# Layer 0 of a two-layer hybrid kernel: one double of seven products fewer, two value blocks beside the attention, deeper mLSTM rings, output weights in the projections' slabs

## The chip, the cores and the metric

The kernel runs on one core of a Trainium2 chip. The metric is the device time of one execution in microseconds (us), as the median of several executions. A profile of one execution has the order and the duration of every instruction on that core.

## What is computed

A backbone of two layers over 1024 latent tokens and 256 context tokens (1280 rows in all, width 1024), in float32. Layer 0 projects the modulated input h by one weight matrix `w_in_ab`, and runs two branches beside each other: 16 heads of neighbourhood attention, and 4 heads of a bidirectional mLSTM. Both are gated, joined and projected out.

```python
def _ab_mixer(h_lat, h_ctx, w_in, ...):
    qa, ka, va, za, qb, kb, vb, ob, zb, g = split(h @ w_in)
    oa_l = _neighbourhood_attention(qa_l, ka_l, va_l, ka_c, va_c, rpb)
    hb_l, hb_c = _mlstm_bidir(mb_l, mb_c, need_ctx)
    ...
    ya = oa * silu(za)
    yb = rms(hb * sigmoid(ob)) * silu(zb)
    return concatenate([ya, yb], -1) @ w_out
```

Layer 1 is a bidirectional gated recurrence (HGRN2) with its own projections. The change is in layer 0 alone; layer 1 takes the profiled execution from about 1900 us on.

## The kernel before, in words

**Precision.** Every float32 operand of a projection is split into a high and a low part (`split`, L72 to L75: ScalarE casts the high part, VectorE subtracts for the low part), and each product is three matmuls (L127 to L129 in `dense`, L743 to L745 in the output projection).

**Blocks.** A projection makes 256 columns at a time. `proj_out` (L269) makes a plain block: 10 token tiles by 8 slices of the depth by 3 matmuls of 128x256, so 240 matmuls; it is called for values (`na_values`), and by `ml_ahead` for the mLSTM's v, o and z. Its output goes through a tile `ev` and a DMA on POOL's queue to DRAM (`vd`, `md`). `q_seven` makes two blocks (a "double") from seven products of half-sized quarters, in Strassen's manner: 7 x 5 x 4 x 3 = 420 matmuls in place of 480, for more work on VectorE.

**Stages of layer 0, in order.** Modulation and h (`hh`, `hl`, kept on chip); gates and a few plain blocks; `a_ahead` with five doubles, the first for the values of attention heads 8 to 15 (the name "n"), the others for q and k of the mLSTM; the attention, in eight passes `p2` of two heads each; the mLSTM (`ml_all`, `ml_rec`), 25 steps g in which head h does its chunk g - 5h, so that one or two heads run at a time; the first half of the output projection's depth (`out_some`), beside the mLSTM; the rest of the output projection with layer 1's norm.

**Fillers.** PE's instructions are issued in program order, and that order is fixed when the program is built: a list scheduler places each instruction by its priority and by a simulated timeline. The plain blocks that nobody needs yet are given beside the attention and the mLSTM, where they stand between the small matmuls of these. Beside the attention this is the table `ahead` (which block after which pass), beside the mLSTM the constants `ML_AHEAD` (block z of head 3 from step 0) and `ML_OUT` (first tile of column half 1 at step 10, of half 0 at step 19, two tiles a step). The context manager `filler` gives them the lowest priority; `tc.issue_after` keeps them behind a certain instruction.

**Memory.** Weight slabs (`w`) and raw loads (`wraw`, 3 buffers) are in the pool `wa` on the right side, behind h. For the output projection `right.close()` at step 9 gives up h and slabs together, and the pool `oy` (weights `wo` in 8 buffers, raws `woraw` in 4, y tiles, accumulators) takes their place. All loads of weights and y tiles go through SP's queue, in order. The ring sizes of `ml_rec` (last argument of `self.t`) set how far a step's work may run ahead.

Of the kernel before, what the change touches and what calls it, by code (L numbers as in the profile page):

```python
# [9 lines left out]
F32 = mybir.dt.float32  # L10
# [8 lines left out]
P = 128  # L19
D = 1024  # L20
# [8 lines left out]
ML_AHEAD = {0: ("z", 3)}  # L29
ML_ORDER = [8, 9, 4, 5, 6, 7, 0, 1, 2, 3]  # L30
ML_OUT = (10, 19)
# [15 lines left out]
class Prog:  # L47
# [400 lines left out]
    def ml_rec(self, h, i, seqs, st, pool):  # L448
        nc = self.nc
        C, hs = st["C"], st["hs"]  # L450
        for d in range(2):
# [11 lines left out]
            if i > 0 or i < NT - 1:  # L463
                cw = self.t(pool, [P, P], F32, "mcw", 2)
                nc.scalar.activation(cw, Gb, AF.Exp, scale=-1.0, bias=self.mpb[:, d, h, i : i + 1])
            if i > 0:
                qc = self.t(pool, [P, 2, P], F32, "mqc", 2)
                nc.vector.tensor_tensor(
                    out=qc, in0=st["q"][c], in1=cw.unsqueeze(1).to_broadcast([P, 2, P]), op=ALU.mult
                )  # L470
                for j in range(2):
                    nc.tensor.matmul(num, lhsT=qc[:, j, :], rhs=C[d][:, j, :], start=False, stop=(j == 1))
            if i < NT - 1:
                vw = self.t(pool, [P, 258], F32, "mvw", 2)
                nc.scalar.activation(vw, st["v"][c], AF.Copy, scale=Dm[:, lastc : lastc + 1])
                us = []
                for j in range(2):
                    u = self.ps("s", [P, 258])
                    nc.tensor.matmul(u, lhsT=st["k"][c][:, j * P : (j + 1) * P], rhs=vw, start=True, stop=True)
                    us.append(u)  # L480
                if i == 0:
                    C[d] = self.t(pool, [P, 2, 258], F32, "mC", 4)
                    for j in range(2):
                        nc.vector.tensor_copy(C[d][:, j, :], us[j])
                else:
                    for j in range(2):
                        nc.vector.scalar_tensor_tensor(
                            out=C[d][:, j, :], in0=C[d][:, j, :], scalar=cw[:, lastc : lastc + 1], in1=us[j],
                            op0=ALU.mult, op1=ALU.add,
                        )  # L490
# [488 lines left out]
    def na_sink(self, b):  # L979
        return lambda c, t, m, o: self.q_store(self.vd[:, (b + c) * 256 : (b + c + 1) * 256], t, m, o)  # L980

# [25 lines left out]
    def a_ahead(self, pool):  # L1007
# [8 lines left out]
        S = {}  # L1016
# [5 lines left out]
        todo = [("n", 2)] + [(p, h) for h in (0, 2) for p in "qk"]  # L1022
        cols = [[2 * D + h * 256 + c * 256 if p == "n" else (4 + "qkvoz".index(p)) * D + (h + c) * 256 for c in range(2)] for p, h in todo]
        sinks = [self.na_sink(h) if p == "n" else self.ml_sink(p, h, pool) for p, h in todo]
        us = [self.q_two(self.q_raw(pool, cols[i], ("11", "21")), S, sinks[i], pool) for i in range(2)] + [None] * 9
# [195 lines left out]
    def build(self):  # L1221
# [3 lines left out]
        with ExitStack() as es:  # L1225
# [92 lines left out]
            wx = right.enter_context(tc.tile_pool(name="wx", bufs=2, side="right"))  # L1318
            self.six = [(self.wp, "w", 4)] * 4 + [(wx, "w", 2)] * 2
            with tc.tile_pool(name="na", bufs=2) as pool, self.pp.phase(tq=1, s=2, acc=1):  # L1320
# [3 lines left out]
                ahead = {2: ["o1"], 3: ["z1"], 4: ["v2"], 5: ["o2"], 6: ["z2"], 7: ["v3", "o3"]}  # L1324
                for p2 in range(8):
# [3 lines left out]
                    for i, x in enumerate(ahead.get(p2, [])):  # L1329
                        with tc.issue_after(self.at[(3, 7)[i]]) if p2 == 7 else nullcontext():  # L1330
                            self.ml_ahead(x[0], int(x[1]))
                    if p2 < 7:
                        z = self.na_z(p2 + 1, pool)
            with tc.tile_pool(name="ml", bufs=2) as pool, self.pp.phase(s=2, acc=2):
                wq = {}
                self.mask = self.t(pool, [P, 2, P], F32, "mmask", 1)
                dma(out=self.mask, in_=a["mmask"])
                wo = lambda q, b, ring, *later: self.wblock(
                    None, "wo", [a["woab"][q * D : (q + 1) * D, b * 512 : b * 512 + 512]], 8, 512, raws, *later, ring=ring
                )  # L1340

                def part(b, tt):
                    self.out_some(wq[b], 0, [tt], self.yd, yp, acc if b else None)

                for g, at in self.ml_all(pool):
                    with self.filler(), tc.issue_after(at.ins):
                        if g in ML_AHEAD:
                            self.ml_ahead(*ML_AHEAD[g])
                        if g == 9:
                            right.close()  # L1350
                            self.six = None
# [3 lines left out]
                            raws = [yp, 4, "woraw"]  # L1355
                        for b, g0 in ((1, ML_OUT[0]), (0, ML_OUT[1])):
                            if g == g0:
                                wq[b] = wo(0, b, [(yp, "wo", 8)] * 8)
                            for tt in ML_ORDER[max(0, 2 * (g - g0)) : max(0, 2 * (g - g0) + 2)]:
                                part(b, tt)  # L1360
                w2 = wo(1, 1, [(yp, "wo", 8)] * 8)
# [8 lines left out]
            with tc.tile_pool(name="op0", bufs=2) as op, ExitStack() as wl:  # L1370
# [13 lines left out]
                wr.close()  # L1384
                right = es.enter_context(ExitStack())
# [213 lines left out]
```

## Time and profile before

| | us |
|---|---|
| median of 3 runs | 3556.39 (3549.15 to 3556.89) |
| the profiled execution | 3552.23 |
| its span, first to last instruction | 3550.4 |
| mean granted TensorE clock | 0.991 |
| 24,318 matmul passes in the span, PE busy | 3466.5 |

The doubles take about 260 to 545 us of the span, the attention about 530 to 1372, the mLSTM 1394 to 1775, the output projection with layer 1's norm runs on to 1904. A matmul of two float32 operands appears in the trace as two passes. PE's busy time counts a pass from its start to its modelled end (0.28 us for 128x256), and passes overlap; what a pass takes of PE is seen from the distance of starts.

### The profile page before, as it was taken

The numbers are of one execution on the slowest core, as the hardware profiler recorded it, in microseconds if no ns is written. First come the engines' busy times: TensorE is split into PE (matmuls) and PEld (weight loads), VectorE is DVE, ScalarE is ACT, GpSimd is POOL, SyncE is SP. The second block draws the span as 40 slices with busy tenths as digits, with TensorE's granted clock in tenths as the row PEclk, the third lists the DMA queues.
The fourth block names the chain that finished last, engine by engine and source line by source line (L and its number), as shares of the span: only waits on it lengthen the run. The fifth ranks groups of instructions, "written<-read, shape, count | busy, mean of one in ns | idle before, by whom it ended". The sixth has DMA issues, their size and how long they took to land.

```text
span 3550.4 us, 64785 instructions
## 1 busy us (share of the span) xinstructions
PE 3466.5 (98%) x24318; PEld 3140.5 (88%) x24318; DVE 2406.6 (68%) x6079; ACT 1596.0 (45%) x3690; POOL 529.2 (15%) x840
## 2 busy tenths in 40 slices
PE   8999999999999999899999999999999999999989
PEld 5899999989999989777878999989999999999877
DVE  4568875776666654667567766577777777767853
ACT  5532224555555543656437333344444444444431
POOL 3211121222222211211211111001000100000010
PEclk9999999999999999999999999999999999999999
DMA  7543342222322224544374222212111211211354
GB/s 236 169 161 98 95 125 61 70 69 69 91 83 77 79 84 142 164 132 144 122 253 150 101 102 102 83 34 60 60 48 51 63 48 48 60 60 48 108 173 126
DMA packets 372681, 359.71 MB, mean 101 GB/s; under 512 B 30104, under 2 KB 322904, under 8 KB 372240
## 3 DMA queue, kind: packets, MB, share of 16 engines
q1 hardware_dynamic: 328944, 248.25, 23.9%
q0 software_dynamic: 43424, 107.32, 8.8%
q8 instruction: 192, 3.15, 0.4%
q14 instruction: 121, 0.99, 0.1%
HBM read 274.00 MB, written 81.32 MB: 100 GB/s over the span
## 4 chain that ended last, share of the span: by engine, by line
PE 84%; issue 5%; DMA 4%; DVE 3%; ACT 2%; POOL 1%; SPq 0%; POOLq 0%; ACTq 0%; DVEq 0%
PE mm L129 14%; PE mm L128 14%; PE mm L127 14%; PE s L1129 6%; PE sa L128 3%; PE sa L127 3%; PE sa L129 3%; PE acc L689 2%; PE mm L743 2%; PE mm L745 2%; PE mm L744 2%; PE tr L669 2%; PE s L1174 1%; PE tr L129 1%; PE tr L128 1%
## 5 line engine op out<-in xcount | busy, mean ns | idle before, releaser
L127 PE MATMUL mm<-wh,hh 128*128 128x256 f32 x1980 | 567.0, 287 | 1.2 <-ACT wh L74 1.1
L128 PE MATMUL mm<-wl,hh 128*128 128x256 f32 x1980 | 567.7, 287 | 0.3 <-DVE wl L75 0.2
L129 PE MATMUL mm<-wh,hl 128*128 128x256 f32 x1980 | 565.6, 286 | 0.0
L129 PE MATMUL mm<-hh,wl 128*128 128x512 f32 (+1 forms) x1344 | 491.0, 365 | 0.0
L127 PE MATMUL mm<-hh,wh 128*128 128x512 f32 (+1 forms) x1344 | 485.2, 361 | 0.0
L128 PE MATMUL mm<-hl,wh 128*128 128x512 f32 (+1 forms) x1344 | 483.9, 360 | 0.0
L127 PEld LDWEIGHTS mm<-wh,hh 128*128 128x128 f32 x1980 | 378.2, 191 | 8.3 <-issue 4.0
L128 PEld LDWEIGHTS mm<-wl,hh 128*128 128x128 f32 x1980 | 378.8, 191 | 4.2 <-DVE wl L75 0.7
L129 PEld LDWEIGHTS mm<-wh,hl 128*128 128x128 f32 x1980 | 378.3, 191 | 3.6 <-issue 1.2
L74 ACT CAST wh<-wraw 128x512 fp32r<-128x512 f32 x272 | 167.3, 620 | 279.3 <-PE mm L128 121.7
L128 PEld LDWEIGHTS mm<-hl,wh 128*128 128x128 f32 x1344 | 254.0, 189 | 32.1 <-issue 0.2
L129 PEld LDWEIGHTS mm<-hh,wl 128*128 128x128 f32 x1344 | 253.9, 189 | 30.2
L127 PEld LDWEIGHTS mm<-hh,wh 128*128 128x128 f32 x1344 | 254.3, 189 | 29.4
L1120 ACT COPY gksel<-gK 128x512 f32<-128x512 f32 x224 | 147.0, 663 | 214.2 <-PE s L1129 205.0
L743 PE MATMUL mm<-woh,yh 128*128 128x512 f32 x544 | 223.0, 410 | 8.3 <-ACT woh L74 4.4
L745 PE MATMUL mm<-woh,yl 128*128 128x512 f32 x544 | 220.0, 405 | 0.2 <-DVE yl L75 0.2
L744 PE MATMUL mm<-wol,yh 128*128 128x512 f32 x544 | 220.2, 405 | 0.0
L75 DVE TENSOR_TENSOR wl<-wraw,wh 128x512 fp32r<-128x512 f32 x272 | 184.4, 687 | 43.7 <-ACT wh L74 38.1
L1129 PE MATMUL s<-gQ,gksel 128*128 128x128 f32 x1536 | 199.8, 276 | 0.0
L1129 PEld LDWEIGHTS s<-gQ,gksel 128*128 128x128 f32 x1536 | 192.4, 191 | 7.0
L74 ACT CAST wh<-b 128x512 fp32r<-128x512 f32 x136 | 84.5, 622 | 209.2 <-PE sa L129 96.2
L1150 DVE TENSOR_TENSOR gQ<-gQ,gT 128x256 f32<-128x256 f32 x384 | 143.7, 416 | 28.0 <-PE s L1129 28.0
(458 smaller groups left out, 8738.0 us busy)
## 6 DMA issues: line engine op xcount, KB each, us to landing
wraw<-yd SPq DMA_DIRECT2D x144, 256.0 KB
wraw<-in_wc_dram SPq DMA_DIRECT2D x128, 256.0 KB
md<-ev POOLq DMA_DIRECT2D x92, 256.0 KB, 2.8
wraw<-in_wab_dram SPq DMA_DIRECT2D x86, 256.0 KB
adar<-in_wada_dram POOLq DMA_DIRECT2D x32, 512.0 KB, 4.8
b<-in_wc_dram SPq DMA_DIRECT2D x64, 256.0 KB
vzd<-qo POOLq DMA_DIRECT2D x56, 256.0 KB, 2.5
b<-in_wab_dram SPq DMA_DIRECT2D x34, 256.0 KB
```

What stands on the lines that cost most here:

```text
L74: nc.scalar.copy(hi, x)
L75: nc.vector.tensor_tensor(out=lo, in0=x, in1=hi.bitcast(F32), op=ALU.subtract)
L127: mm(ps, lhsT=lh(k), rhs=rh(k), start=(first and k == 0), stop=False)
L128: mm(ps, lhsT=lh(k), rhs=rl(k), start=False, stop=False)
L129: mm(ps, lhsT=ll(k), rhs=rh(k), start=False, stop=(last and k == nk - 1))
L669: nc.tensor.transpose(pt[:nk, i, :], pr[:, o : o + nk], self.ident)
L743: mm(ps, lhsT=yh[:, k, :], rhs=w.h(kk), start=(kk == 0), stop=False)
L744: mm(ps, lhsT=yh[:, k, :], rhs=w.l(kk), start=False, stop=False)
L745: mm(ps, lhsT=yl[:, k, :], rhs=w.h(kk), start=False, stop=(kk == 8 * len(qs) - 1))
L1120: nc.scalar.copy(ksel.rearrange("p (b s i) -> p b s i", s=2, i=h), pick(K))
L1129: nc.tensor.matmul(pa[:, c, :].rearrange("p (b s i) -> p b s i", s=2, i=h), lhsT=ksel[:, c * P : (c + 1) * P], rhs=qp[:, c * nbc : (c + 1) ...
L1150: nc.vector.tensor_tensor(out=t[:, i, :, s, :], in0=t[:, i, :, s, :], in1=bc(tot), op=ALU.mult)
```

## The change

Six things change, all in layer 0.

1. `a_ahead` makes four doubles in place of five: the double of values ("n", 2) goes.
2. The values of blocks 2 and 3 (heads 8 to 15) are made as plain blocks, after passes 1 and 2 of the attention. The other fillers move back by one or two passes; o of head 3 moves from pass 7 into the mLSTM.
3. `ML_AHEAD`: o3 from step -1, z3 from step 2 (before: z3 from step 0). `ML_OUT` becomes a list of steps for every tile: half 1 from step 8 to 12, half 0 from step 13 to 24.
4. Rings of `ml_rec`: E 2 to 3, Dm 3 to 5, SD, cw, qc and vw 2 to 4.
5. The pool `wa` is opened below h, so that h is given up alone (`rh.close()`, at step 7 in place of 9). The slabs live on to the end of the output projection, and output weights go into a ring of 11 places: 4 slabs `w` and 7 `wo`; their raws into `wraw` (3 buffers).
6. The extra slabs `wx` stand on the left side beside the attention's pool.

```diff
-ML_AHEAD = {0: ("z", 3)}
+ML_AHEAD = {-1: ("o", 3), 2: ("z", 3)}
-ML_OUT = (10, 19)
+ML_OUT = {1: (8, 8, 9, 9, 10, 10, 11, 11, 12, 12), 0: (13, 14, 14, 15, 16, 17, 18, 20, 22, 24)}
...
-            E = self.t(pool, [P, P], F32, "mE", 2)
+            E = self.t(pool, [P, P], F32, "mE", 3)
-            Dm = self.t(pool, [P, P], F32, "mD", 3)
+            Dm = self.t(pool, [P, P], F32, "mD", 5)
-            SD = self.t(pool, [P, P], F32, "mSD", 2)
+            SD = self.t(pool, [P, P], F32, "mSD", 4)
...
-        todo = [("n", 2)] + [(p, h) for h in (0, 2) for p in "qk"]
+        todo = [(p, h) for h in (0, 2) for p in "qk"]
...
-            self.open_h(right)
             self.wp = right.enter_context(tc.tile_pool(name="wa", bufs=2, side="right"))
+            rh = right.enter_context(ExitStack())
+            self.open_h(rh)
...
-                ahead = {2: ["o1"], 3: ["z1"], 4: ["v2"], 5: ["o2"], 6: ["z2"], 7: ["v3", "o3"]}
+                ahead = {1: ["n2"], 2: ["n3"], 3: ["o1"], 4: ["z1"], 5: ["v2"], 6: ["o2"], 7: ["z2", "v3"]}
...
-                        with tc.issue_after(self.at[(3, 7)[i]]) if p2 == 7 else nullcontext():
-                            self.ml_ahead(x[0], int(x[1]))
+                        with tc.issue_after(self.at[(3, 6)[i]]) if p2 == 7 else nullcontext():
+                            self.na_values(int(x[1])) if x[0] == "n" else self.ml_ahead(x[0], int(x[1]))
...
-                wq = {}
+                wq, self.six = {}, [(self.wp, "w", 4)] * 4
+                with self.filler(), tc.issue_after(self.at[8]):
+                    self.ml_ahead(*ML_AHEAD[-1])
...
+                def wo(q, b, ring=None):
+                    if not ring:
+                        ring, self.six = self.six[:8], self.six[8:] + self.six[:8]
+                    src = a["woab"][q * D : (q + 1) * D, b * 512 : b * 512 + 512]
+                    return self.wblock(None, "wo", [src], 8, 512, ring=ring)
...
-                        if g == 9:
-                            right.close()
-                            self.six = None
+                        if g == 7:
+                            rh.close()
...
+                            self.six = self.six + [(yp, "wo", 7)] * 7
...
-                w2 = wo(1, 1, [(yp, "wo", 8)] * 8)
+                w2 = wo(1, 1)
...
                 wr.close()
+                right.close()
+                self.six = None
```

What it moves is seen in the order of instructions. On PE, at the end of the second attention pass (p2 = 1), these rows stood in a row before; `s` are scores, `tr` and `tq` transposes, `acc` the attention's sums, and a projection would be `mm`:

```order
L619 MATMUL s_9112<-akh_8602,aqs_8600 128x256
L620 MATMUL s_9112<-akl_8604,aqs_8600 128x256
L669 MATMUL tr_9100<-ident_73,aP_9082 96x128 x2
L669 MATMUL tr_9100<-ident_73,aP_9082 72x128
L557 MATMUL tq_9922<-ident_73,aqn_9915 128x128 x4
L669 MATMUL tr_9106<-ident_73,aP_9082 128x128 x2
L632 MATMUL s_9117<-akh_8602,aqs_8600 128x264
L633 MATMUL s_9117<-akl_8604,aqs_8600 128x264
L619 MATMUL s_9157<-akh_8601,aqs_8599 128x256
L620 MATMUL s_9157<-akl_8603,aqs_8599 128x256
```

In the changed program the end of the same pass reads so on PE (`mm_9648` is the q and k projection of a later pass, which now has its turn here since the block n2 was done earlier in the pass):

```order
L669 MATMUL tr_7892<-ident_73,aP_7870 96x128 x3
L128 MATMUL mm_9648<-wl_9464,hh_126 128x256
L669 MATMUL tr_7897<-ident_73,aP_7870 128x128 x2
L619 MATMUL s_7931<-akh_6843,aqs_6841 128x256
L620 MATMUL s_7931<-akl_6845,aqs_6841 128x256
L129 MATMUL mm_9648<-wh_9465,hl_127 128x256
L127 MATMUL mm_9648<-wh_9472,hh_126 128x256
L128 MATMUL mm_9648<-wl_9471,hh_126 128x256
L662 MATMUL acc_7889<-ident_73,arb_7887 128x128
```

The stretch without a projection, 67 rows long before (rows 5544 to 5611 of PE), is gone there. At the start of the last pass such a stretch stays, and goes from 89 rows (9080 to 9169) to 66 (8920 to 8986).

On PE, in the mLSTM, these rows are out of a stretch of 126 (10129 to 10255) that held no filler before; `num` is `acc`, `s` is a score or an update of the state, `tr` a transpose:

```order
L479 MATMUL s_19156<-mvw_19154,mkn_3104_18221 128x258
L479 MATMUL s_19158<-mvw_19154,mkn_3104_18221 128x258
L526 MATMUL tr_19178<-ident_73,mhs_3164_18374 128x128
L472 MATMUL acc_19227<-mC_18640,mqc_19231 128x258 x2
L394 MATMUL tr_19191<-ident_73,mqn_19189 128x128 x2
L479 MATMUL s_19237<-mvw_19235,mkn_3403_19004 128x258
L479 MATMUL s_19239<-mvw_19235,mkn_3403_19004 128x258
L400 MATMUL tr_19198<-ident_73,mkn_3475_19196 128x128 x2
```

In the changed program the same update of the state (its `mkn` has the number 18998 here) stands between matmuls of a tile of the output projection (`mm_19334`):

```order
L744 MATMUL mm_19334<-wol_19328,yh_19335 128x512
L462 MATMUL acc_19412<-mv_3004_17797,mSD_19410 128x258
L472 MATMUL acc_19412<-mC_17742,mqc_19416 128x258
L526 MATMUL tr_19177<-ident_73,mhs_3133_18368 128x128
L472 MATMUL acc_19412<-mC_17742,mqc_19416 128x258
L462 MATMUL acc_19449<-mv_2997_17779,mSD_19447 128x258
L526 MATMUL tr_19132<-ident_73,mhs_3144_18396 128x128
L472 MATMUL acc_19449<-mC_17767,mqc_19453 128x258
L479 MATMUL s_19238<-mvw_19234,mkn_3372_18998 128x258
L472 MATMUL acc_19449<-mC_17767,mqc_19453 128x258
L479 MATMUL s_19264<-mvw_19262,mkn_3379_19016 128x258
L745 MATMUL mm_19334<-woh_19329,yl_19336 128x512
```

Before, two long stretches of the mLSTM stood without a filler (126 and 118 rows, the second 10600 to 10718). In the changed program the longest is 37 rows (10229 to 10266), and fourteen shorter ones of 10 to 30 rows lie between there and the end of the mLSTM.

On SP's queue, where the output projection starts, this stood before; `gbc` is a row of gates that goes into the pool `oy`, and so waits until h is given up:

```order
L428 DMA mGb_3316_18764<-Gd_67 128x512 x2
L790 DMA gbc_22651<-gated_63 128x512 x2
L389 DMA mv_3399_18993<-md_72 128x256
L103 DMA woraw_19630<-in_woab_dram 128x512
L103 DMA woraw_19636<-in_woab_dram 128x512
L103 DMA woraw_19642<-in_woab_dram 128x512
L103 DMA woraw_19648<-in_woab_dram 128x512
L730 DMA wraw_19679<-yd_65 128x4x128
L730 DMA wraw_19683<-yd_65 128x4x128
```

In the changed program three of the weight loads stand some 30 rows ahead of it, and the rest about it:

```order
L103 DMA wraw_19306<-in_woab_dram 128x512
L790 DMA gbc_22643<-gated_63 128x512
L515 DMA mlz_19168<-md_72 128x256
L790 DMA gbc_22643<-gated_63 128x512
L103 DMA wraw_19312<-in_woab_dram 128x512
L103 DMA wraw_19318<-in_woab_dram 128x512
L415 DMA mkn_3445_19195<-md_72 128x256
L730 DMA wraw_19337<-yd_65 128x4x128
L730 DMA wraw_19341<-yd_65 128x4x128
```

More of the change, by code (lines that the diff above doesn't have):

```diff
@@ L1317, in build @@
                 self.a_ahead(pool)
-            wx = right.enter_context(tc.tile_pool(name="wx", bufs=2, side="right"))
-            self.six = [(self.wp, "w", 4)] * 4 + [(wx, "w", 2)] * 2
-            with tc.tile_pool(name="na", bufs=2) as pool, self.pp.phase(tq=1, s=2, acc=1):
+            with tc.tile_pool(name="na", bufs=2) as pool, tc.tile_pool(name="wx", bufs=2) as wx, self.pp.phase(tq=1, s=2, acc=1):
+                self.six = [(self.wp, "w", 4)] * 4 + [(wx, "w", 2)] * 2
                 qk = self.na_qk(0, pool)
```

30 lines of the change are left out of this document (11 added, 19 removed).

## The prediction

> **What bounds the kernel now.** I read the page's table of engines first, then the busy time by stretch, then the groups of PE and the order of time in the stretches that stand out.
>
> ```profile
> PE 3466.5 (98%) x24318; PEld 3140.5 (88%) x24318; DVE 2406.6 (68%) x6079; ACT 1596.0 (45%) x3690; POOL 529.2 (15%) x840
> ```
>
> PE bounds the kernel; VectorE (DVE) and ScalarE (ACT) have room on the mean. But 98% is no measure of what is left, since passes overlap. So I count passes by stretch. The columns are the stretch in us, its length, busy us and count for PE, PEld, DVE, ACT and POOL, then the granted clock and DMA.
>
> ```profile
> 350.00:400.00 50.00, 50.00 (x424) 50.00 (x422) 41.38 (x84) 10.14 (x17) 8.03 (x12) 1.00 0.31 96
> 740.00:780.00 40.00, 40.00 (x368) 38.66 (x366) 25.19 (x84) 18.52 (x52) 9.04 (x12) 1.00 0.25 66
> 780.00:812.00 32.00, 26.55 (x200) 22.56 (x201) 24.97 (x88) 19.54 (x59) 8.52 (x11) 0.84 0.26 79
> 812.00:850.00 38.00, 38.00 (x305) 34.68 (x300) 25.68 (x80) 21.06 (x55) 7.70 (x11) 1.00 0.36 99
> 1240.00:1288.00 48.00, 48.00 (x401) 44.18 (x399) 30.26 (x97) 23.33 (x64) 8.29 (x12) 1.00 0.28 81
> 1288.00:1313.00 25.00, 18.00 (x130) 13.41 (x127) 16.13 (x70) 9.06 (x33) 5.51 (x9) 0.86 0.34 97
> 1395.00:1460.00 65.00, 63.03 (x444) 59.08 (x445) 31.87 (x105) 30.98 (x89) 6.91 (x15) 1.00 0.44 140
> 1460.00:1533.00 73.00, 60.28 (x289) 46.51 (x288) 57.91 (x201) 50.27 (x151) 19.60 (x51) 0.95 0.66 206
> 1533.00:1633.00 100.00, 99.59 (x473) 82.40 (x472) 62.77 (x190) 57.77 (x153) 16.57 (x50) 1.00 0.45 132
> 1633.00:1698.00 65.00, 56.97 (x278) 44.23 (x277) 51.09 (x180) 44.08 (x134) 14.05 (x38) 0.97 0.47 145
> 1698.00:1780.00 82.00, 80.65 (x373) 66.24 (x372) 46.05 (x128) 40.26 (x103) 19.66 (x37) 1.00 0.40 125
> 1780.00:1800.00 20.00, 15.95 (x60) 11.74 (x60) 9.90 (x19) 8.16 (x15) 0.58 (x1) 0.91 0.98 319
> 1900.00:1950.00 50.00, 46.51 (x349) 44.85 (x348) 35.54 (x77) 32.46 (x93) 7.08 (x14) 0.93 0.35 117
> ```
>
> The doubles (350 to 400) run without a gap: 424 passes in 50 us, 118 ns each for 128x256. Where a projection stands between the attention's or the mLSTM's small matmuls (740, 812, 1240, 1533, 1698) PE has no gap worth a name. Layer 0 loses its time in five holes: 780 to 812, 1288 to 1313, 1460 to 1533, 1633 to 1698, 1780 to 1800. In the first four the order of before has no projection on PE. So PE stands where fillers have run out, and this is what the change is to be measured by: PE work added against holes filled.
>
> **The doubles and the plain blocks.** A double goes, 420 passes; two plain blocks come, 480. Both are 128x256 passes of the same kind, so 60 x 118 ns = **+7.1 us** of PE, wherever they stand. The double also had 14 casts and 14 subtractions of 128x512 for its seven weight forms, 8 additions and the recombination; two plain blocks need 8 of each, no recombination, and 10 evictions on ACT and 10 stores on POOL's queue. DVE and ACT get lighter. Between 350 and 400 both lie under PE, so I give this nothing. The 8 weight loads on SP replace 8 of the double. The stores stand on POOL ahead of the attention's loads of values; the store of the block z1, v2 or o2 did so before, and 1240 to 1288 has no gap with it: nothing. If that cover failed, it would show as a hole like the one at 780, +10.6.
>
> **The attention.** At 780 to 812 PE is idle for 32 - 26.55 = 5.45 us, and the clock of 0.84 takes 0.16 x 32 = 5.1 more: 10.6 us. This is the end of the second pass, and the waits there are the softmax chain's:
>
> ```profile
> 784.47 0.43 PE L669 MATMUL tr<-ident,aP 128*128 128x128 f32 x2
> 786.01 0.30 PE L662 MATMUL acc<-ident,arb 128*128 128x128 f32 x1 [1.10 <-DVE az L706]
> ```
>
> The order of the changed program has projections all through this place, as in 812 to 850, which has no idle time. So **-10.6**; its 200 passes at the 109 ns a pass of 740 to 780 (40 us by 368) would take 21.7 us and leave 10.3, so the two ways agree. Bounds 0 (the chain waits all the same) and -10.6. At 1288 to 1313, 7.0 us idle and 0.14 x 25 = 3.5 of clock, 10.5 in all; the run of rows without projection goes from 89 to 66, so a quarter comes back: **-2.7**, bounds 0 and -10.5.
>
> The Trainium skill ("TensorE: Matmul & The Clock Gate", part 1 on the clock gate) says that the clock is halved after an idle window of about 3.4 us; here it shows 0.84 in a stretch whose longest single wait of PE is the 1.10 us quoted. By that rule the clock would not be lost in such a hole, and the term at 780 would be 5.5 in place of 10.6; by the row it is 10.6, and the row decides.
>
> **The mLSTM.** What the passes of the long hole cost is read from a dense stretch just ahead of it (start, modelled length, passes) and from the groups of PE in the hole (count | busy, mean | idle before):
>
> ```profile
> 1454.97 0.60 PE L407 MATMUL s<-mqT,mkT 128*128 128x128 f32 x4
> 1455.41 0.60 PE L462 MATMUL acc<-mv,mSD 128*128 128x258 f32 x2
> 1455.85 1.03 PE L472 MATMUL acc<-mC,mqc 128*128 128x258 f32 x4
> 1456.72 0.61 PE L407 MATMUL s<-mqT,mkT 128*128 128x128 f32 x4
> ```
>
> ```profile
> L479 PE MATMUL s<-mvw,mkn 128*128 128x258 f32 x74 | 21.6, 399 | 1.1 <-DVE mC L487 0.6 <-ACT mvw L475 0.5
> L472 PE MATMUL acc<-mC,mqc 128*128 128x258 f32 x72 | 20.6, 412 | 0.4 <-DVE mqc L468 0.4
> L462 PE MATMUL acc<-mv,mSD 128*128 128x258 f32 x43 | 12.8, 386 | 0.3 <-ACT mhs L501 0.3
> L407 PE MATMUL s<-mqT,mkT 128*128 128x128 f32 x40 | 6.3, 280 | 1.3 <-ACT mST L409 1.3
> L526 PE MATMUL tr<-ident,mhs 128*128 128x128 f32 x20 | 5.6, 296 | 6.0 <-ACT myt L527 4.7 <-DVE mhs L522 0.7 <-DMA mlo<-md 0.5
> L394 PE MATMUL tr<-ident,mqn 128*128 128x128 f32 x20 | 4.3, 301 | 2.9 <-DMA mqn<-md 1.7 <-ACT myt L527 1.2
> L400 PE MATMUL tr<-ident,mkn 128*128 128x128 f32 x20 | 4.0, 283 | 0.7 <-ACT mkT L402 0.4 <-ACT mqT L396 0.2
> ```
>
> Four passes of 128x258 take 1456.72 - 1455.85 = 0.87 us, 217 ns each; four of 128x128 take 0.44, 110 each. The hole has 189 of the first and 100 of the second: 41.0 + 11.0 = 52.0 us of work in 73, so 21.0 are lost. At the same 180 ns a pass, the 278 of 1633 to 1698 are 50.0 of 65: 15.0 lost. The mixed stretches (1395, 1533, 1698) are idle for 2.0 + 0.4 + 1.3 = 3.7. So the mLSTM loses about **39.7** us.
>
> In the changed order the fillers are spread. One run of 37 rows without filler is left of 126, at the point where h is given up: 21.0 x 37/126 = 6.2. The rest, some 370 us with o3's 240 passes, I price at the worst of the mixed rows, 1395 to 1460: 2.0/65 = 3%, 11 us, since its fourteen short runs are more than 1533 to 1633 had. Left 17, so **-22.7**. Bounds: if all 228 rows of the short runs went at the long hole's rate, 38 + 6 would be lost, +4; if they cost what 1533 to 1633 costs (0.4%), 1.5 + 6 are left, -32. I take 3%, as these rows are nearest in kind. The deeper rings are what lets the work stand so; they add no instruction, and DVE at 58 of 73 us in the hole has room to go beside fillers (its work in 1395 to 1780 sums to 250 us of 385).
>
> Part of the long hole is a queue's. SP held the gates' row until h was free, with loads behind it; a weight cast then waited at the head of ACT, and PE for ACT:
>
> ```profile
> 1471.22 0.62 ACT L74 CAST woh<-woraw 128x512 fp32r<-128x512 f32 x1 [2.81 <-DMA woraw<-in_woab_dram]
> ```
>
> ```profile
> 1474.40 0.33 PE L526 MATMUL tr<-ident,mhs 128*128 128x128 f32 x1 [3.78 <-ACT myt L527]
> ```
>
> Slabs that live on need not wait for h, and three weight loads now stand ahead of that row; the y loads still wait. This is within the 21.0.
>
> **Seam after the mLSTM.** 1780 to 1800 is idle for 4.05 and loses 0.09 x 20 = 1.8: 5.9 us, when all eight weights wait for the last tile of half 0. Now six of eight loads stand ahead, and the order has the next tile's first nine matmuls before the last tile's end: **-4**, bounds 0 and -5.9. The seams where pools change places elsewhere (`wx` to the left, slabs closed later ahead of layer 1) I cost at nothing: the earlier one ends the doubles, where PE has no gap, and the later keeps the loss that 1900 to 1950 shows now (3.5 idle, 3.5 clock). If one of them fails, +6 to +7, the price of such a seam.
>
> **Sum.** 7.1 - 10.6 - 2.7 - 22.7 - 4 = -32.9, against the profiled execution's 3552.2 us (span 3550.4): **3519**. The median of the runs shown is 4.2 higher, within their spread of 7.7; I leave that in the range.
>
> **Rivals.**
> - *The holes move.* The order is spread, but in the mLSTM's late steps one or two heads feed DVE and ACT chains, and the short runs wait at the long hole's rate. For it: DVE 79% busy in the hole. Against it: 1533 to 1633 has short runs too and 0.4 us idle. Then the mLSTM's and the seam's terms are about 0: 3552.2 + 7.1 - 13.3 = 3546; with half the mLSTM term, 3535.
> - *Only waits come back.* The passes of holes are slow for their own dependences, and the clock stays. Idle time alone: 5.5, 1.8, (12.7 + 8.0) x 22.7/39.7 = 12, 2.8; so 3552.2 + 7.1 - 22 = 3537. The clock-gate rule of the Trainium skill (above) makes the attention's terms come out so.
> - *More comes back.* The mixed rows' 0.4% holds for all the mLSTM and the last pass's hole closes: 3552.2 + 7.1 - 10.6 - 10.5 - 32 - 6 = 3500; runs that come out 4 us under the profiled one, as the spread of before allows, make it 3496.
> - *Slower: casts at the head of ACT.* The 16 output weights of the mLSTM share three raw buffers, and 40 casts of y stand in ACT's order all through steps 8 to 24 in place of two groups. Where the DMA is later than the builder's timeline had it, ACT stands, and PE after it, 3.8 us at 1474. With nine such stalls of the 56 casts the gain of 32.9 is gone, with fourteen the time is 3572. For it: that row. Against: between 1533 and 1633 some 9 tiles were cast among the mLSTM with 0.4 us of idle PE in all.
>
> **How the numbers follow.** Forecast (3505 to 3530): 0.52. More comes back (3492 to 3505): 0.13. Only waits, or half the mLSTM term (3530 to 3545): 0.18. Holes move, within 7 us of before (a difference of 0.2%, about what a measurement of this kernel can tell from no change): 0.08. Slower by more: 0.09. Faster 0.83, same 0.08, slower 0.09. The range, 3496 to 3543, leaves out the slower cases, the unchanged one and a few hundredths at the low end.
>
> **What would show it.** No stretch with a clock under 0.9 between 700 and 800 less the 50 us that the doubles lose; a hole of some 20 us left at the start of the last pass; PE busy for 97% or more of the mLSTM from the first output tile on, and one short run of it without filler ahead of that. Wrong if the mLSTM's part shows ACT waiting for `wraw` at the head of its queue with PE idle behind it, or if DVE is over 90% busy there.

## The result, and the profile after

| | before | changed kernel |
|---|---|---|
| median, 20 runs each, side by side (us) | 3555.68 (3549.15 to 3559.69) | 3549.61 (3541.76 to 3553.77) |
| ratio to before, 95% interval | | 0.9984 (0.9977 to 0.9991) |
| profiled execution (us) | 3552.23 | 3541.76 |
| its span (us) | 3550.4 | 3539.9 |

The change gains 6 us by the medians and 10.5 between the two profiled executions, where the forecast had 33. The time lies outside its range.

I place the difference by the same instructions in both traces: the first matmul of the doubles (`sa`), the first transpose of the attention's normalised q (`aqn`), the last matmul of the output projection ahead of layer 1. In between I count as the prediction did: the length of a stretch, less its passes at the spacing of a dense stretch (119 ns for 256 columns, 217 for 258, 229 for 512, 110 for 128, 96 for transposes, 53 for the attention's paired ones). What remains is called lost.

| stretch | before | changed | length differs by |
|---|---|---|---|
| start to first `sa` | 0 to 259.8 | 0 to 256.7 | -3.1 |
| doubles, to first `aqn` | to 532.3, 5.3 lost | to 495.5, 21.5 lost | -33.7 (420 passes fewer) |
| attention and mLSTM, to the last output tile | to 1903.5 | to 1895.1 | +28.4 (480 passes more) |
| of it lost in the attention, the mLSTM, the seam | 68.9, 45.9, 7.0 | 53.3, 34.0, 5.3 | |
| layer 1, to the end | to 3550.4 | to 3539.9 | -2.1 |

The 420 passes of a double are worth 49.6 us at 118 ns, and only 33.7 came: 16 us were given back there. The two plain blocks are 56.6 us, and the stretch grew by 28.4: 28 us were won there, 16 in the attention and 12 to 14 in the mLSTM with its seam. Then 7.1 + 16 - 28 = -5, and the start and layer 1, where nothing was changed, differ by 5 more. That part is no more than the spread between executions: in eight kernels that are alike up to the doubles the first `sa` comes between 256.7 and 262.2, and layer 1 takes 1642 to 1650 us in the fourteen traces.

**The doubles.** The table of engines reads as before:

```profile
PE 3460.8 (98%) x24378; PEld 3144.3 (89%) x24378; DVE 2390.2 (68%) x6044; ACT 1597.8 (45%) x3691; POOL 524.6 (15%) x838
```

By stretch (columns as in the prediction) before and the changed kernel part company at 300 us. Before:

```profile
280.00:300.00 20.00, 17.59 (x130) 16.54 (x130) 17.82 (x30) 5.36 (x10) 0.00 (x0) 0.94 0.11 27
300.00:320.00 20.00, 20.00 (x166) 19.93 (x165) 18.27 (x33) 5.79 (x10) 0.57 (x1) 0.97 0.22 60
320.00:340.00 20.00, 20.00 (x170) 19.94 (x170) 15.94 (x30) 3.72 (x6) 6.03 (x9) 1.00 0.51 159
```

The changed kernel:

```profile
280.00:300.00 20.00, 17.22 (x130) 15.59 (x129) 18.35 (x29) 4.45 (x8) 0.00 (x0) 1.00 0.11 27
300.00:320.00 20.00, 17.55 (x139) 16.61 (x138) 17.05 (x35) 3.72 (x6) 2.58 (x4) 1.00 0.28 85
320.00:340.00 20.00, 15.69 (x108) 15.28 (x107) 18.10 (x36) 3.62 (x6) 2.71 (x4) 0.83 0.25 81
340.00:360.00 20.00, 17.14 (x140) 16.56 (x139) 15.34 (x34) 2.48 (x4) 3.48 (x6) 1.00 0.42 122
```

Idle time there is 12.4 us and the clock loses 3.4 more. PE's waits between 280 and 360 in the changed kernel (releaser, us in total, times, longest) begin so:

```profile
PE sa L127 <- DVE qu L956: 3.5, 1, 3.5
PE sa L127 <- DVE ev L932: 1.8, 1, 1.8
PE sa L128 <- DVE wl L75: 1.4, 3, 0.8
```

These are releases by VectorE, and so is the rest but for 1.9 us by ScalarE's cast `hh` of the sums (2.0 before). VectorE still makes the last sums and their splits (`qs`, `hl`) and the weight forms (`wl`), and now the first double rotates q as well (the rope), where before the rope began with the second. These are the two largest groups of the rope between 280 and 360, in the changed kernel and before:

```profile
L999 DVE TENSOR_TENSOR qs<-ev,mrope 128x512 f32<-128x512 f32 x8 | 5.5, 686 | 0.1
L1000 DVE TENSOR_TENSOR ev<-ev,mrope 128x512 f32<-128x512 f32 x7 | 4.8, 683 | 0.0
```

```profile
L1002 DVE TENSOR_TENSOR qs<-ev,mrope 128x512 f32<-128x512 f32 x4 | 2.7, 684 | 0.0
L1003 DVE TENSOR_TENSOR ev<-ev,mrope 128x512 f32<-128x512 f32 x3 | 2.1, 687 | 0.0
```

All groups of the rope take 23 us of VectorE in these 80 us, 11 before, while VectorE is busy for nearly the same time in all (68.8 and 67.5): work that PE waits for is done later. VectorE's own waits for the stores of `ev` hardly differ (7.0 us, 6.4 before).

**The attention** came as forecast, and a little more. The hole at 780 is gone, and the one at the start of the last pass, now at 1256, keeps 2.8 idle and 1.8 of clock where 10.5 were lost:

```profile
740.00:780.00 40.00, 40.00 (x368) 38.44 (x367) 30.05 (x97) 22.89 (x61) 10.76 (x13) 1.00 0.25 73
780.00:812.00 32.00, 32.00 (x292) 31.06 (x291) 21.69 (x71) 18.00 (x50) 8.50 (x13) 1.00 0.30 83
1256.00:1282.00 26.00, 23.16 (x167) 19.11 (x165) 15.74 (x58) 9.57 (x29) 3.33 (x5) 0.93 0.34 103
```

**The mLSTM** has no long hole any more; it loses a little everywhere, and a few us at single places:

```profile
1440.00:1480.00 40.00, 39.97 (x267) 37.08 (x267) 29.29 (x95) 21.15 (x61) 8.96 (x29) 1.00 0.39 117
1480.00:1505.00 25.00, 19.04 (x83) 15.06 (x83) 20.33 (x64) 17.33 (x49) 5.30 (x11) 0.86 0.92 281
1505.00:1605.00 100.00, 97.46 (x474) 80.92 (x473) 60.67 (x187) 56.49 (x155) 17.06 (x50) 1.00 0.45 133
1605.00:1700.00 95.00, 88.94 (x428) 73.09 (x427) 61.25 (x195) 55.34 (x157) 18.28 (x48) 0.98 0.51 154
1700.00:1791.00 91.00, 87.25 (x411) 70.20 (x411) 62.60 (x183) 48.45 (x135) 23.33 (x44) 1.00 0.45 141
```

Its three longest waits of PE, in order of time:

```profile
1487.15 0.33 PE L526 MATMUL tr<-ident,mhs 128*128 128x128 f32 x1 [2.44 <-ACT myt L527]
1489.71 0.69 PE L394 MATMUL tr<-ident,mqn 128*128 128x128 f32 x2 [2.23 <-ACT myt L527]
1614.08 1.23 PE L479 MATMUL s<-mvw,mkn 128*128 128x258 f32 x2 [3.64 <-ACT mST L409]
```

The engine named, ACT, does its part (`myt`, `mST`) a moment before. What held ACT stands ahead of it in ACT's order:

```profile
1485.55 1.27 ACT L74 CAST woh<-wraw 128x512 fp32r<-128x512 f32 x2 [2.75 <-DMA wraw<-in_woab_dram]
1486.73 0.36 ACT L527 ACTIVATE myt<-tr,hnb 128x128 f32<-128x128 f32 x1
...
1488.77 0.62 ACT L74 CAST yh<-wraw 128x512 fp32r<-128x512 f32 x1 [1.28 <-DMA wraw<-yd]
1489.29 0.36 ACT L527 ACTIVATE myt<-tr,hnb 128x128 f32<-128x128 f32 x1
...
1611.20 0.62 ACT L74 CAST wh<-wraw 128x512 fp32r<-128x512 f32 x1 [4.08 <-DMA wraw<-in_woab_dram]
```

Each time a cast waits for its load, and a copy that PE needs stands behind it. This is what the prediction named as the sign of the rival "casts at the head of ACT", and as a sign that it is wrong. From the first output tile to the end of the mLSTM (1505 to 1791) PE is busy for 96% of the time, where the prediction asked for 97%.

### The profile page after: what moved, and what is told of

Its sections match the earlier page's. It is cut to its first block, busy times and chain, and to the rows that moved or that the text cites. A ratio compares the mean times of both kernels' runs of the same rounds, so it can differ in the third digit from the quotient of the medians.

```text
span 3539.9 us, 64788 instructions
## 1 busy us (share of the span) xinstructions
PE 3460.8 (98%) x24378; PEld 3144.3 (89%) x24378; DVE 2390.2 (68%) x6044; ACT 1597.8 (45%) x3691; POOL 524.6 (15%) x838
## 4 chain that ended last, share of the span: by engine, by line
PE 81%; issue 9%; DMA 3%; DVE 2%; ACT 2%; POOL 1%; SPq 0%; POOLq 0%; ACTq 0%; DVEq 0%
PE mm L129 14%; PE mm L127 14%; PE mm L128 14%; PE s L1126 6%; PE acc L689 2%; PE tr L669 2%; PE sa L128 2%; PE sa L127 2%; PE sa L129 2%; PE acc L472 2%; PE s L479 1%; PE s L1171 1%; PE mm L743 1%; PE mm L744 1%; PE mm L745 1%
## 5 line engine op out<-in xcount | busy, mean ns | idle before, releaser
L127 PE MATMUL mm<-wh,hh 128*128 128x256 f32 x2120 | 608.1, 287 | 2.4 <-ACT ev L545 1.5
L128 PE MATMUL mm<-wl,hh 128*128 128x256 f32 x2120 | 608.4, 287 | 0.7 <-DVE wl L75 0.7
L129 PE MATMUL mm<-wh,hl 128*128 128x256 f32 x2120 | 608.4, 287 | 0.4 <-DVE hl L75 0.4
L127 PEld LDWEIGHTS mm<-wh,hh 128*128 128x128 f32 x2120 | 404.6, 191 | 9.9 <-issue 3.7
L128 PEld LDWEIGHTS mm<-wl,hh 128*128 128x128 f32 x2120 | 404.8, 191 | 5.1 <-DVE wl L75 0.9
L129 PEld LDWEIGHTS mm<-wh,hl 128*128 128x128 f32 x2120 | 404.4, 191 | 5.3 <-issue 1.5
L743 PE MATMUL mm<-woh,yh 128*128 128x512 f32 x444 | 180.2, 407 | 6.1 <-ACT woh L74 3.3
L745 PE MATMUL mm<-woh,yl 128*128 128x512 f32 x444 | 177.9, 401 | 1.0 <-DVE yl L75 0.9
L744 PE MATMUL mm<-wol,yh 128*128 128x512 f32 x444 | 177.7, 400 | 0.0
```

Of the source, the lines that this page charges most:

```text
L127: mm(ps, lhsT=lh(k), rhs=rh(k), start=(first and k == 0), stop=False)
L128: mm(ps, lhsT=lh(k), rhs=rl(k), start=False, stop=False)
L129: mm(ps, lhsT=ll(k), rhs=rh(k), start=False, stop=(last and k == nk - 1))
L743: mm(ps, lhsT=yh[:, k, :], rhs=w.h(kk), start=(kk == 0), stop=False)
L744: mm(ps, lhsT=yh[:, k, :], rhs=w.l(kk), start=False, stop=False)
L745: mm(ps, lhsT=yl[:, k, :], rhs=w.h(kk), start=False, stop=(kk == 8 * len(qs) - 1))
```

## The experiments

Three are on the doubles, seven on the mLSTM, and two are versions that beat both kernels. Edits are to the changed kernel where nothing else is said. All were timed in turns with the kernel before on the same chip, so ratios are to be compared (the changed kernel: 0.9984). "Lost" is counted as above.

| kernel | median us | ratio (95%) | lost: doubles | attention | mLSTM | seam |
|---|---|---|---|---|---|---|
| before | | 1 | 5.3 | 68.9 | 45.9 | 7.0 |
| changed kernel | 3549.6 | 0.9984 (0.9977 to 0.9991) | 21.5 | 53.3 | 34.0 | 5.3 |
| five doubles | 3542.4 | 0.9968 (0.9955 to 0.9980) | 5.6 | 69.7 | 38.8 | 5.4 |
| z0 ahead of the sums | 3538.1 | 0.9957 (0.9943 to 0.9970) | -0.1 | 56.1 | 42.6 | 6.6 |
| no rope in the first double | 3530.5 | 0.9939 (0.9927 to 0.9951) | 7.7 | 52.2 | 35.9 | 5.7 |
| old rings | 3543.8 | 0.9973 (0.9963 to 0.9982) | 24.5 | 53.3 | 33.4 | 2.2 |
| dense tiles | 3546.8 | 0.9978 (0.9968 to 0.9987) | 27.5 | 56.6 | 37.2 | 0.3 |
| dense tiles, old rings | 3548.7 | 0.9982 (0.9972 to 0.9992) | 25.1 | 53.4 | 39.4 | 0.3 |
| old rings, own raws | 3548.0 | 0.9977 (0.9966 to 0.9988) | 24.9 | 56.3 | 35.5 | 2.4 |
| one set of weights | 3542.4 | 0.9962 (0.9951 to 0.9974) | 24.4 | 53.1 | 29.6 | 5.8 |
| o3 beside the attention, z3 at 0 | 3561.5 | 1.0015 (1.0006 to 1.0024) | 26.6 | 52.6 | 46.3 | 5.3 |
| z3 at 0 | 3548.7 | 0.9986 (0.9977 to 0.9994) | 24.3 | 52.6 | 34.2 | 4.2 |
| z0 ahead, old rings, own raws | 3529.5 | 0.9932 (0.9919 to 0.9944) | -0.1 | 64.5 | 30.8 | 3.3 |
| the same, last blocks earlier | 3528.9 | 0.9925 (0.9913 to 0.9937) | -0.1 | 55.1 | 40.6 | 2.3 |

### Five doubles again

```diff
-        todo = [(p, h) for h in (0, 2) for p in "qk"]
+        todo = [("n", 2)] + [(p, h) for h in (0, 2) for p in "qk"]
...
-                ahead = {1: ["n2"], 2: ["n3"], 3: ["o1"], 4: ["z1"], 5: ["v2"], 6: ["o2"], 7: ["z2", "v3"]}
+                ahead = {2: ["o1"], 3: ["z1"], 4: ["v2"], 5: ["o2"], 6: ["z2"], 7: ["v3"]}
```

> The changed kernel with its first part undone: five doubles again, the one of the last heads' values first, and no plain block of values beside the attention; the spread attention order keeps the six blocks that are left, and the whole mLSTM part stays as changed. Theory (the four doubles have a hole of their own, 280 to 360 us, 16 us lost, since the first of them now has a rope on VectorE while VectorE still makes the sums): the hole is gone, PE does 7.1 us less, and the attention loses 10 to 16 us more because its fillers run out again; together 0 to 13 us less than the changed kernel, about 3542 us. Rival, the forecast's own view (doubles cost nothing beside PE, the whole shortfall lies in the mLSTM): the doubles gain nothing and the attention loses 13: about 6 us slower than the changed kernel, 3556 us. Either way the stretch from the last attention to the end should stay within 2 us of the changed kernel's.

Measured: 0.9968, as the theory had it. The hole of the doubles is gone (3.7 us idle in these 80, 2.4 before), and the attention loses what it lost before. The same stretch as above:

```profile
280.00:360.00 80.00, 76.35 (x628) 74.87 (x627) 66.75 (x119) 18.52 (x31) 10.03 (x15) 1.00 0.33 100
```

So the change without its first part gains 11 us, and with it 6: taking the values out of the doubles costs 5 to 6 us as it was made, though the intervals just overlap. By the terms: 7.1 of PE work and 16 to 22 in the doubles, against 16 in the attention and 5 in the mLSTM. The stretch after the attention did not stay within 2 us, as I had expected: its loss rose by 5. With one block fewer in the last pass, 298 projection passes stand between the first and the last matmul of the mLSTM, where the changed kernel has 424 (the next run has 298 too, and loses 42.6).

### z of head 0 ahead of the sums

```diff
         self.ml_ahead("o", 0, True)
+        self.ml_ahead("z", 0, True)
         S["1"] = a21
...
-                self.ml_ahead("z", 0)
-                ahead = {1: ["n2"], 2: ["n3"], 3: ["o1"], 4: ["z1"], 5: ["v2"], 6: ["o2"], 7: ["z2", "v3"]}
+                ahead = {0: ["n2"], 1: ["n3"], 2: ["o1"], 3: ["z1"], 4: ["v2"], 5: ["o2"], 6: ["z2"], 7: ["v3"]}
```

> The changed kernel with the plain block z of head 0 (240 passes, no rope) made ahead of the doubles' sums in place of the start of the attention, and the plain blocks beside the attention one pass earlier each. Theory (VectorE makes the sums, the weight forms and the first rope at once and PE stands for it): VectorE gets some 28 us of PE time to do the sums under, the hole of 280 to 360 shrinks from 16 us to under 5, and the time falls by 8 to 13 us, to about 3538. Rival (the hole is that of the two-buffer store of the rows, or of the weight loads): it stays in the first double, wherever that starts: within 2 us of the changed kernel.

Measured: 0.9957, 10 us less. PE has no gap left in that stretch, with the rope, the stores and the loads all still there:

```profile
280.00:360.00 80.00, 80.00 (x673) 80.00 (x672) 71.33 (x131) 22.79 (x39) 9.48 (x14) 1.00 0.31 93
```

The doubles start 37 us later in this run, and lose nothing in all their length (-0.1 in the table). VectorE is even busier than in the changed kernel (68.84 of 80 there). It is not VectorE's load on the mean that made the hole, but that it came when PE had nothing else to do. Part of the 21 us won went back in the mLSTM (42.6 for 34.0), which lost a block at its border, and in the attention (56.1 for 53.3).

### No rope in the first double

```diff
-            if part in "qk" and t < LAT // P:
+            if part in "qk" and (part, h) != ("q", 0) and t < LAT // P:
```

> The changed kernel with the rotation of q left out for the first double (heads 0 and 1), so that this part of the computation is not done; stores and loads stay as they are. Theory (rope on VectorE in the first double makes the hole): 8 to 14 us less, the loss of the stretch 280 to 360 falls under 6 us. Rival (stores, buffers of the rows or weight loads make it): the hole stays, within 2 us of the changed kernel.

Measured: 0.9939, 16 us less, some more than expected; the hole falls from 12.4 us of idle time to 2.7:

```profile
280.00:360.00 80.00, 77.34 (x626) 76.15 (x626) 67.15 (x119) 17.96 (x30) 10.02 (x15) 0.98 0.34 104
```

The stores through two buffers and the weight loads are still there, the hole is not. Its cause is the first double's rope on top of the sums: with either of the two out of the way, here the rope and in the run before this one the sums, the hole is gone.

### Old rings

```diff
-            SD = self.t(pool, [P, P], F32, "mSD", 4)
+            SD = self.t(pool, [P, P], F32, "mSD", 2)
```

and likewise for the other five.

> The changed kernel with the mLSTM's six rings at their old depth, and the order as the scheduler then makes it. Theory (the short runs are bound by their chains through VectorE and ScalarE, which deeper rings let overlap): the stretch from the first to the last mLSTM instruction grows by 5 to 15 us, nothing changes ahead of 1357 us. Rival (rings are no bound; casts and loads at the head of a queue make what is lost): within 2 us of the changed kernel.

Measured: 0.9973, 4 us less than the changed kernel and so nearer the rival's answer, but outside the 2 us that it allowed. The mLSTM loses 33.4 for 34.0 and the seam 2.2 for 5.3. The deeper rings give nothing. The scheduler's order differs too, with 480 projection passes beside the mLSTM for 424, so this run does not part the rings from the order that comes with them.

### Dense tiles, and dense tiles with old rings

```diff
-ML_OUT = {1: (8, 8, 9, 9, 10, 10, 11, 11, 12, 12), 0: (13, 14, 14, 15, 16, 17, 18, 20, 22, 24)}
+ML_OUT = {1: (10, 10, 11, 11, 12, 12, 13, 13, 14, 14), 0: (19, 19, 20, 20, 21, 21, 22, 22, 23, 23)}
```

> The changed kernel with the ten output tiles of each half put back to two a step in steps 10 to 14 and 19 to 23, as before, everything else as changed. If the forecast's step is right that spreading the fillers is what gives in the mLSTM (12.6 us were got there), the stretch from the last attention to the last output tile loses 10 to 15 us more, and the time is about 3559 us. Rival (the order hardly matters, what is lost are stalls of ScalarE's queue on casts whose load is late, and those are there in any order): within 4 us of the changed kernel, 3546 to 3554 us.

> Output tiles two a step in steps 10 to 14 and 19 to 23, as before, and the old ring depths: of the mLSTM's change there is left only where o and z of head 3 stand, the slabs that outlive h, and the eleven slabs. Dense tiles alone gave 3546.8 us and old rings alone 3543.8, beside 3549.6 of the change as made. If neither the rings nor the spread order give anything: 3542 to 3550 us, 35 to 42 us lost from the last attention to the last output tile. If each hides the lack of the other (deep rings help where the order is dense): 50 us lost there, 3555 to 3560 us.

Measured: 0.9978 and 0.9982, both beside the changed kernel's 0.9984: the spread order gives nothing either, with deep rings or without. Where the loss lies does change. With dense tiles and old rings the two holes of before are back, and the seam is closed:

```profile
1480.00:1540.00 60.00, 50.38 (x265) 39.29 (x264) 42.59 (x137) 39.45 (x113) 12.91 (x28) 0.97 0.63 196
...
1640.00:1725.00 85.00, 77.43 (x367) 60.93 (x368) 61.25 (x212) 55.62 (x164) 17.72 (x44) 0.96 0.41 127
1725.00:1780.00 55.00, 55.00 (x253) 45.35 (x252) 32.28 (x89) 24.63 (x66) 15.03 (x29) 1.00 0.42 132
1780.00:1830.00 50.00, 50.00 (x223) 41.31 (x221) 36.71 (x60) 22.70 (x39) 5.14 (x9) 1.00 0.96 312
```

From the last attention to the last output tile this order loses 39.7 us, the spread one 39.3. What the spread order wins in the holes it loses in the short runs (1605 to 1791), at the casts and in the seam, where tiles were left until step 24.

### Own raw buffers

```diff
-                    return self.wblock(None, "wo", [src], 8, 512, ring=ring)
+                    return self.wblock(None, "wo", [src], 8, 512, *raws, ring=ring)
...
+                            raws = [rw.enter_context(tc.tile_pool(name="orw", bufs=1, side="right")), 4, "woraw"]
...
```

on top of the old rings.

> Output weights get four raw buffers of their own again, in place of the three that they share with the loads of y; the old ring depths make the room for it, so the kernel to compare with is the one with old rings (3543.8 us, 33.4 us lost from the last attention to the last mLSTM instruction). Theory (casts stand at the head of ScalarE because a load must first wait for one of three shared raws): the stalls of PE at 1484, 1487 and 1610 us (2.6, 2.5 and 3.8 lost) go, 5 to 9 us less: about 3537 us. Rival (the loads wait for slabs or for the queue, not for raws): those stalls stay, within 2 us of the kernel with old rings.

Measured: 0.9977, and 35.5 lost in the mLSTM for 33.4: the rival's answer. ACT still meets a cast whose load is late. Behind that cast stand four more (one of them waits 0.42 us for its load) ahead of the copy `mkT`, for which PE waits 3 us:

```profile
1616.23 0.62 ACT L74 CAST woh<-woraw 128x512 fp32r<-128x512 f32 x1 [1.76 <-DMA woraw<-in_woab_dram]
```

```profile
1621.14 0.44 PE L400 MATMUL tr<-ident,mkn 128*128 128x128 f32 x2 [3.02 <-ACT mkT L402]
```

SP's queue suggests why more raw buffers don't help: the next weight loads are issued behind two loads of y, after a pause of 6 us.

```profile
1602.98 0.32 SPq L515 DMA_DIRECT2D mlz<-md  x1
1609.44 0.97 SPq L730 DMA_DIRECT2D wraw<-yd  x2
1611.05 0.34 SPq L103 DMA_DIRECT2D woraw<-in_woab_dram  x1
```

That the order of SP's queue is the bound there is read from these rows; no run moved it.

### One set of output weights

```diff
-                                wq[b] = wo(0, b)
+                                wq[b] = wo(0, b) if b else wq[1]
```

> The changed kernel with the second half's output tiles computed from the first half's weights, so that one half of this partial output is not the right one: eight loads, eight casts on ScalarE and eight subtractions at step 13 of the mLSTM are left out, the loads and casts of y and all of PE's work stay. Theory (casts at the head of ScalarE, whose load is late, hold PE): the stall of 3.8 us at 1610 goes and the stretch 1595 to 1640 loses 4 to 7 us less, the time falls by as much, to about 3544 us; the two stalls at 1484 and 1487 stay. Rival (the stretch's loss is that of the short runs' own chains): within 2 us.

Measured: 0.9962, 7 us less. The same matter in the changed kernel, from 1595, and here, from 1600:

```profile
1595.00:1640.00 45.00, 40.84 (x194) 33.29 (x193) 29.44 (x85) 27.86 (x77) 8.64 (x22) 0.96 0.60 178
```

```profile
1600.00:1645.00 45.00, 44.05 (x216) 36.59 (x215) 27.72 (x86) 25.92 (x74) 8.26 (x22) 1.00 0.47 144
```

PE's wait for ScalarE's `mST` falls to 0.5 us there, and the two ahead of it stay (2.45 and 2.21 us), as expected. So the eight casts at step 13, with their loads and subtractions, cost 4 to 7 us: the rival of the casts is real. These eight give about a fifth of the 33 us that it needed to undo the gain; the other casts were not taken out.

### o and z of head 3 back where they stood

```diff
-ML_AHEAD = {-1: ("o", 3), 2: ("z", 3)}
+ML_AHEAD = {0: ("z", 3)}
...
-                ahead = {1: ["n2"], 2: ["n3"], 3: ["o1"], 4: ["z1"], 5: ["v2"], 6: ["o2"], 7: ["z2", "v3"]}
+                ahead = {1: ["n2"], 2: ["n3"], 3: ["o1"], 4: ["z1"], 5: ["v2"], 6: ["o2"], 7: ["z2", "v3", "o3"]}
...
```

> The changed kernel with the plain block o of head 3 (240 passes, 28 us of PE) put back to the end of the attention and z of head 3 to step 0 of the mLSTM, as before; the spread output tiles stay. Theory (filler at the mLSTM's start is what fills the first half of its old hole): the stretch from the last attention to the last output tile loses 8 to 12 us more in the steps ahead of the first output tile, the hole at the start of the last attention pass shrinks by up to 5, together about 3554 us. Rival (where these blocks stand is of no account, what counts is that the slabs outlive h and the weights come early): within 3 us of the changed kernel, some 3550 us.

Then the second of the two moves alone (`ML_AHEAD = {-1: ("o", 3), 0: ("z", 3)}`):

> The changed kernel with the block z of head 3 back at step 0 of the mLSTM, where it stood before, and o of head 3 left ahead of the mLSTM. The two moves undone together cost 12 us in the run with o beside the attention. If o of head 3 at the mLSTM's start is what gave it: within 3 us of the changed kernel, about 3550 us. If it is z two steps later that fills the steps ahead of the first output tile: the hole there grows from 10 to 18 us lost and the time is 3557 to 3560 us.

Measured: 1.0015 and 0.9986. The place of z gives nothing; the place of **o of head 3** gives 11 us, nearly all that the mLSTM gained (12). The groups of PE between the last attention matmul (1364.3) and the first of the mLSTM (1406.9), with o3 beside the attention:

```profile
L129 PE MATMUL mm<-wh,hl 128*128 128x256 f32 x118 | 33.5, 284 | 0.0
L128 PE MATMUL mm<-wl,hh 128*128 128x256 f32 x117 | 33.1, 283 | 0.0
L127 PE MATMUL mm<-wh,hh 128*128 128x256 f32 x117 | 33.1, 283 | 0.0
```

These are 352 passes of plain blocks in a row (one block has 240) with nothing beside them: the attention is over, the mLSTM has not begun, and PE is busy all the time. In the kernel before, 112 such passes stand between the last attention matmul (1380.2) and the first of the mLSTM (1393.9):

```profile
L129 PE MATMUL mm<-wh,hl 128*128 128x256 f32 x38 | 10.9, 286 | 0.0
L128 PE MATMUL mm<-wl,hh 128*128 128x256 f32 x37 | 10.5, 283 | 0.0
L127 PE MATMUL mm<-wh,hh 128*128 128x256 f32 x37 | 10.5, 283 | 0.0
```

With o3 put back, the mLSTM then runs out of filler, at the old hole's place:

```profile
1460.00:1530.00 70.00, 60.60 (x295) 48.05 (x294) 51.38 (x175) 45.03 (x129) 14.46 (x41) 0.93 0.60 181
```

The attention loses the same with o3 there (52.6) and without (53.3). A block that stands at the end of a stage covers nothing, and shows as a PE without a gap. Between the first and the last matmul of the mLSTM there are 240 projection passes in this run, as before the change (46.3 and 45.9 lost), and 424 in the changed kernel and with z3 at 0 (34.0 and 34.2 lost).

### The versions that beat both

The first has z0 ahead of the sums, old rings, own raws and the blocks at passes 0, 2 to 6 and two at 7; the second issues the last two after `self.at[1]` and `self.at[5]` in place of 3 and 6.

> Old rings and own raw buffers as in the run beside it, and the plain block z of head 0 ahead of the doubles' sums, with the attention's eight blocks at passes 0, 2, 3, 4, 5, 6 and two in 7. If the two gains add up (about 10 from the doubles, 5 to 9 from the raws): 3528 to 3533 us, the fastest of all that compute everything. If the raws give nothing: about 3537 us.

> The fastest version so far (z of head 0 ahead of the doubles' sums, old rings, own raw buffers; 3529.5 us) with the two blocks of the last attention pass issued after its second and sixth iteration in place of the fourth and seventh. Theory (the hole at the start of the last pass is only a lack of filler): it loses 8 to 11 us less at 1250 to 1300, and if nothing opens later the time is 3519 to 3522 us. Rival (the blocks' weight loads wait for slabs, or the hole opens again at the pass's end): within 3 us, 3527 to 3533 us.

Measured: 0.9932, then 0.9925. The first is 24 us under before by the medians, and its span is 3526.8 for 3550.4. Old rings and own raws gave 2 to 4 us at most by themselves, so most of its gain beside the changed kernel is that of z0 and of where the blocks stand. In the second the hole at the start of the last pass shrinks as expected, from the first row to the second:

```profile
1243.00:1290.00 47.00, 40.84 (x309) 34.21 (x308) 26.89 (x110) 17.71 (x58) 5.96 (x9) 0.85 0.25 72
```

```profile
1243.00:1290.00 47.00, 43.65 (x377) 39.60 (x376) 27.30 (x105) 17.28 (x55) 7.48 (x11) 1.00 0.27 79
```

but the attention's 9.4 us (64.5 to 55.1) come back in the mLSTM, whose loss goes from 30.8 to 40.6: part of what filled the one hole is missing in the other (386 projection passes beside the mLSTM, for 480). The rival was right.

## Why the prediction was wrong, point by point

- **PE work, +7.1**: right. It is the difference of 480 and 420 passes, and they run at 118 to 119 ns in both.
- **Doubles at nothing**: this step failed. "Both lie under PE" was read from 350 to 400, the middle of the stage, where it still holds. It failed in the first double, where the sums are made. The double that was taken out was the one without a rope there, and gave VectorE the time for them; I counted its casts and subtractions as relief and did not ask what stands in its place. Shown by three runs: the hole goes with the values back, with the rope out, or with other PE work ahead. Price 16 to 22 us, where the text had 0, and +10.6 if the cover failed.
- **Attention, -10.6 and -2.7**: right in mechanism, and near in size, 16 for 13.3; the hole of the last pass gave 5.9 for 2.7. In the trace of before, the place without a projection ends at 801, not at 812 as the text reads it, which changes no term. The hole at 780 gave its idle time and its clock, so the row decided rightly. By the rule of the Trainium skill ("TensorE: Matmul & The Clock Gate", part 1), that the clock is halved after an idle window of about 3.4 us, 5.5 of the 10.6 would have come. The changed kernel again shows a clock of 0.86, between 1480 and 1505, with no wait above 2.44 us. Its hole in the doubles fits that rule: the clock of 0.83 between 320 and 340 comes with a wait of 3.50 us.
- **mLSTM, -22.7**: 12 came, and not from what I said. The spread order, priced at 3% in the short runs, was the second step that failed: dense tiles lose as much up to the last output tile (39.7 for 39.3). The short runs at 1605 to 1791 are idle for 6.1 + 3.8 of 186 us, 5%, and the place at 1480 loses 9.5 for 6.2. The 12 us come from the place of o3, which the text counted only as passes in the stretch. That projection passes can stand where they cover nothing was to be seen in the trace of before (the 112 passes after 1380.2), and no stretch that the prediction counted began or ended there. The change did not free these: 168 stand alone at that place in the changed kernel, and 352 with o3 put back. It won by giving the mLSTM more filler. What the 34 us that it still loses are made of is shown for the casts at step 13 alone.
- **Rings**: "what lets the work stand so". No run shows any worth of them.
- **Seam, -4**: 1.7 came. With the eleven slabs and dense tiles it does close (0.3 lost), as the text argued, but the spread order leaves tiles at its end that open it again.
- **Rivals**: "the holes move" with half the mLSTM term (3535) describes the mLSTM best. Its full form, 3546, lies near the time that came, but by luck: it had no loss in the doubles and no gain in the mLSTM. "Casts at the head of ACT" is real, at 4 to 7 us for the eight that were tried. None looked at the doubles, where 16 us went.

Not settled: why the start of the same code differs by over 5 us between executions, and why the loss in the doubles is 21.5 in the profiled execution of the change and 24 to 28 in seven kernels with the same doubles.

## What to carry to other kernels

When an instruction block is taken out of a sequence, look at what it was cover for at its own place, not at the stage's mean: the stage's first and last elements have neighbours that the middle has not. Filler is worth what the stretch beside it lacks; a block that runs alone at a stage's end shows a PE without a gap, and is the one to move, while moving one that already fills a hole only moves the hole. Before spreading an order or deepening rings, ask what holds the instruction ahead of the waiting one on its own queue: here, in the three longest waits, it was a cast behind a load, and neither touched it.
